# Half B's last projection interleaved, token tile by token tile, with steps of half A's channel mixer; attention outputs stored from ScalarE's queue

## The chip, the cores and the metric

The kernel runs on one NeuronCore of a Trainium2 chip. The metric is the device time of one execution in microseconds (us), the median of several runs. Five instruction streams run side by side and meet only at semaphores: PE (TensorE, the matrix multiplies), DVE (VectorE), ACT (ScalarE), POOL (GpSimd) and SP (SyncE, which here issues all data transfers). Each stream is executed in the order in which the program lists it.

## The reference, cut to what matters

A two-layer trunk is applied to 1024 prompt rows and 64 sample rows of width 1024. Each layer is a mixer, then a gated feed-forward block (the "channel mixer"), each with a residual and a layer norm:

```python
x = layer_norm(DEEPNORM_ALPHA * x + mix, ln1_w[layer], ln1_b[layer])
x = layer_norm(DEEPNORM_ALPHA * x + swiglu(x, ffn_w_in[layer], ffn_w_out[layer]), ln2_w[layer], ln2_b[layer])

def swiglu(x, w_in, w_out):
    gate, up = jnp.split(x @ w_in, 2, axis=-1)      # 1024 -> 2 x 2816
    return (jax.nn.silu(gate) * up) @ w_out         # 2816 -> 1024
```

Layer 0's mixer is a recurrent one, layer 1's is chunk-band softmax attention with 16 heads of 64, whose output goes through one projection, `mix = attention(x) @ w_o` (1024 x 1024). The change lies wholly in layer 1.

## The kernel before, in words

**Two halves.** The rows are split into half A (384 prompt rows and the 64 sample rows, 448 columns, index 0) and half B (the other 640 prompt rows, index 1, five token tiles of 128). The halves run out of step, so that the vector work of one lies beside the matrix work of the other. In layer 1, half A is already in its channel mixer while half B is in attention.

**Precision.** Every product is made of three matmuls: operands are kept as a rounded high part and a low part (`wh`/`wl` for a weight, `xh`/`xl` for an activation), and hi*hi, hi*lo and lo*hi are summed. `load_w` (L93 to 108) loads a weight of 512 KB into a raw buffer `wr` (two of them), ACT rounds it to `wh` (L100), and DVE and POOL share the subtraction that gives `wl` (L105, L107). There are four buffers each for `wh` and `wl` (`self.WB = 4`).

**Channel mixer of half A.** `ffn` (L906) is a Python generator. Each step j of 22 loads two weights, runs 2 x 24 matmuls of 128x448 (`gemm_ws`, L123 to L125), and forms one hidden tile `hh`/`hl`. After steps 3, 7, 11, 15, 17 and 21 (`GROUPS`), the hidden tiles so far go through the output matrix (`tsg`), whose matmuls are 128x512 and whose sums DVE adds into `acc` (L823, L825). `next(f)` asks for one step more.

**Projection of half B.** `proj` runs `tsg` twice, for the second and then the first half of the inner dimension. Each `tsg` has two column halves (nh) of 512, and per token tile and nh 12 matmuls (L134, L135, L137). The second `tsg` got `after`, the layer norm of a tile: it loaded all four of its weights first, and then ran tile by tile both column halves and `after(i)`.

**Layer norm.** Per tile: DVE takes statistics (L871, L873), POOL forms the reciprocal deviation `rstd` (L875, L876), DVE scales (L879, L884 for the second column half), ACT and POOL finish the first column half (L881, L882), and PE transposes both halves, four 128x128 blocks each (L889). Then `sums` (L950 to 1003) splits the transposed tile into high and low parts and builds, on DVE and ACT, the operand sums S1 to S4 that half B's own channel mixer (`s_ffn`) multiplies; that mixer computes two row halves in a form with fewer products.

**Order.** The program is recorded and then scheduled by a planner: every engine gets a fixed list, mainly in the order of the code, with later work pulled ahead where the planner's model sees an engine free. Buffers are given out in that order too. At the end of layer 1's attention of half B, `run` (L1455 to 1469) goes on with `for j in f`; at j = 15 (`JM`) it loads the attention outputs `og_d` and the residual, and calls `self.proj(1, acc1, "w_o", ...)`. Steps 16 to 21 of half A's mixer come after it, then `s_ffn`. The attention of a pair of heads ends with its output tile `o` (DVE, L1312) stored to `og_d` from SP's queue (L1316).

Of the kernel before, what the change touches and what calls it, by code (L numbers as in the profile page):

```python
# [82 lines left out]
class Kern:  # L83
# [712 lines left out]
            self.nc.sync.dma_start(acc[i][:m], src[self.base[hf] + t0 : self.base[hf] + t0 + m, :])  # L796
        return acc

    def tsg(self, hf, acc, wsrc, pairs, hi, lo, first, after=None, packed=None):

        def load(nh):
            ws = []
            for pr in pairs:
                h_, l_ = self.load_w(wsrc(nh, pr), [128, 2, 512])
                ws += [(h_[:, j, :], l_[:, j, :]) for j in range(2)]
            return ws

        kts = [2 * pr + j for pr in pairs for j in range(2)]  # L810

        def part(ws, nh, i, t0, m):
            two = packed and m == 64
            ps = self.bank()
            if two:
                self.gemm_ts(ps, ws, packed, None, kts, lambda x: x[:, 0:128])
            else:
                self.gemm_ts(ps[:m], ws, hi, lo, kts, lambda x: x[:, t0 : t0 + m])
            a = acc[i][:m, 512 * nh : 512 * nh + 512]
            if first:  # L820
                self.V.scalar_tensor_tensor(a, a, ALPHA, ps[:m], op0=ALU.mult, op1=ALU.add)
            else:
                self.V.tensor_tensor(a, a, ps[:m], op=ALU.add)  # L823
            if two:
                self.V.tensor_tensor(a, a, ps[m:], op=ALU.add)  # L825

        if after is None:
            for nh in range(2):
                ws = load(nh)
                for i, t0, m in self.toks(hf):  # L830
                    part(ws, nh, i, t0, m)
        else:
            ws = [load(nh) for nh in range(2)]
            for i, t0, m in self.toks(hf):
                for nh in range(2):
                    part(ws[nh], nh, i, t0, m)
                after(i)
# [6 lines left out]
        self.G.tensor_copy(xs[:, :, 64:128], xt.lo[:, :, SMP:])  # L844
        return lambda kt: xs[:, kt, :]

    def proj(self, hf, acc, wname, after, pool=None):

        xt = self.xt[hf]
        packed = self.pack(pool) if pool else None  # L850
        for i, g in enumerate((1, 0)):
            self.tsg(hf, acc, lambda nh, pr: self.a[wname][nh, pr], (2 * g, 2 * g + 1), xt.h, xt.l, i == 0, after if i else None, packed)

    def layer_norm(self, hf, acc, which, layer, out=None, transpose=True, sums=None):

# [347 lines left out]
    def attention(self, hf, hp, sp, parts=None):  # L1203


        nc, V, A, G, T = self.nc, self.V, self.A, self.G, self.T
        n, xt, c0 = self.N[hf], self.xt[hf], self.base[hf]
# [14 lines left out]
        o = sp.tile([128, n], F32, tag="o", name="o", bufs=1)  # L1222
# [6 lines left out]
        for h in range(2):  # L1229
# [18 lines left out]
            for grp in groups:  # L1248
                ng, first = len(grp), grp[0][2][0][0]
# [5 lines left out]
                for i, (q0, m, keys) in enumerate(grp):  # L1255
# [21 lines left out]
                    for j0 in range(0, len(keys), 4):  # L1277
# [10 lines left out]
                        for dst, src, kk in ops:  # L1288
                            t3 = tp[:kk].rearrange("p (j q) -> p j q", q=128)[:, src, :m]
                            hi = ph[:kk, dst, :m]  # L1290
# [22 lines left out]
        if hf == 0:  # L1313
            self.split(xt.h(hp), xt.l(hp), o)
        else:
            nc.sync.dma_start(self.og_d[hp], o)  # L1316


    def run(self):
        nc, tc, a = self.nc, self.tc, self.a  # L1320
# [26 lines left out]
        g = self.gla(0, sc, 1, None)  # L1347
# [25 lines left out]
        g = self.gla(1, sc, 1, gS)  # L1373
# [9 lines left out]
        hp = es_a.enter_context(tc.tile_pool(name="hpA", bufs=1))  # L1383
# [21 lines left out]
        with tc.tile_pool(name="qp", bufs=1) as qp:  # L1405
            self.vproj(0, qp, 2)
            for hp in range(8):
                if hp == self.JX:
                    with tc.tile_pool(name="yr1", bufs=1, side="right") as yp:
                        self.load_xt(1, self.yg_d, (4, 5, 6, 7, 0, 1, 2, 3), pool=yp)  # L1410
                    acc1 = self.load_acc(1, a["x"], accp)
# [9 lines left out]
        hp = es_b.enter_context(tc.tile_pool(name="hpB", bufs=1))  # L1421
        f = self.ffn(1, 0, acc1, hp, lambda: self.layer_norm(1, acc1, "ln2", 0, xd(1)))
# [11 lines left out]
        with tc.tile_pool(name="at1", bufs=1, side="right") as atp:  # L1434
# [13 lines left out]
            hp = es_a.enter_context(tc.tile_pool(name="hpA1", bufs=1))  # L1448
            outA = lambda t0, m: a["y_s"] if t0 == SMP else a["y_p"][t0 : t0 + m, :]
            f = self.ffn(0, 1, acc0, hp, lambda: self.layer_norm(0, acc0, "ln2", 1, outA, transpose=False))  # L1450
# [7 lines left out]
        for j in f:  # L1458
            if j == self.JM:
                accp = self.ctx.enter_context(tc.tile_pool(name="accB1", bufs=1, side="right"))  # L1460
                self.xt[1] = self.xt_tiles(xbp, 1)
                with tc.tile_pool(name="yr2", bufs=1, side="right") as yp:
                    self.load_xt(1, self.og_d, (4, 5, 6, 7, 0, 1, 2, 3), pool=yp)
                self.paired = True
                acc1 = self.load_acc(1, self.x_d, accp)
                xs, sums = self.s_operands(self.ctx.enter_context(tc.tile_pool(name="sx", bufs=1, side="right")),
                                           self.ctx.enter_context(tc.tile_pool(name="st", bufs=1, side="right")))
                self.proj(1, acc1, "w_o", self.layer_norm(1, acc1, "ln1", 1, sums=sums))
        es_a.close()
        hp = self.ctx.enter_context(tc.tile_pool(name="hpB1", bufs=1))  # L1470
        outB = lambda t0, m: a["y_p"][PA + t0 : PA + t0 + m, :]
# [86 lines left out]
```

## Time and profile before

| what | value |
|---|---|
| median of 3 runs | 3194.87 us (3192.62 to 3196.44) |
| the profiled execution | 3194.15 us, of which the span from first to last instruction is 3192.4 us |
| PE busy | 3038.5 us, 95% of the span |
| DVE, POOL, ACT busy | 2029.7, 1342.5, 1263.7 us |
| mean granted TensorE clock | 0.968 of full speed |
| end of half B's attention (last L1307 matmul) | about 2486 us |
| half B's projection with its layer norm | about 2549 to 2647 us |
| steps 16 to 21 of half A's mixer | about 2647 to 2739 us |
| first matmul of half B's mixer (L1044) | 2749.7 us |

The page cuts the span into 40 slices of 79.8 us; a digit is a busy share in tenths, and the row PEclk is the clock that TensorE was granted. Stages named here by time can be looked up there: slices 30 and 31 hold the end of the attention, slice 32 the projection.

### The profile page before, as it was taken

The page shows a single profiled execution, that of the slowest core. Times are in us where ns is not written, and L with a number is a line of the kernel's source. Part 1 is how long each engine was busy: PE and PEld are TensorE (multiplying, and loading weights), DVE is VectorE, ACT ScalarE, POOL GpSimd, SP SyncE. Part 2 cuts the span into 40 slices and gives each one's busy share as a digit, 9 for nine tenths or more (in the row PEclk, how much of TensorE's full clock was granted, in tenths as well). Part 3 has the DMA queues.
Part 4 walks back from the last instruction along what each step waited for, and adds up shares of the span by engine and source line. Part 5 has one row for each costly group of instructions (what it writes and reads, how often), then busy time and mean ns, then how long its engine had stood idle before and what let it go on. Part 6 is the DMA issues. An engine that isn't in the chain of part 4 may idle for free.

```text
span 3192.4 us, 50089 instructions
## 1 busy us (share of the span) xinstructions
PE 3038.5 (95%) x17468; PEld 2695.8 (84%) x17468; DVE 2029.7 (64%) x4953; ACT 1263.7 (40%) x2753; POOL 1342.5 (42%) x1461
## 2 busy tenths in 40 slices
PE   8999998899999999999999999999997979899998
PEld 7878887688888878888899898999996858799987
DVE  4677885979888664555553635445665556766667
ACT  4454553434444324244342223454444323333332
POOL 2354433535454334343332323345455323555444
PEclk9989999799999999999999999999997889999999
DMA  6553444434433248344432325764543413322121
GB/s 194 145 156 110 113 119 111 142 102 122 134 103 109 88 151 271 112 135 119 119 97 93 108 74 197 210 193 147 146 130 98 142 34 113 108 86 100 54 93 73
DMA packets 297341, 395.10 MB, mean 124 GB/s; under 512 B 125377, under 2 KB 218425, under 8 KB 297089
## 3 DMA queue, kind: packets, MB, share of 16 engines
q1 hardware_dynamic: 297088, 391.90, 41.1%
q8 instruction: 138, 2.26, 0.3%
q14 instruction: 115, 0.93, 0.1%
HBM read 319.44 MB, written 75.51 MB: 124 GB/s over the span
## 4 chain that ended last, share of the span: by engine, by line
PE 76%; DVE 9%; DMA 6%; issue 4%; POOL 3%; ACT 2%; SPq 1%; POOLq 0%; DVEq 0%; ACTq 0%
PE gps L123 11%; PE gps L124 11%; PE gps L125 11%; PE gps L134 7%; PE gps L135 7%; PE gps L137 6%; PE gps L1044 2%; PE gps L1045 2%; PE gps L1046 2%; PE op L1307 2%; PE tp L1281 2%; DVE x L550 1%; PE sps L1265 1%; DVE t L548 1%; PE ps L621 1%
## 5 line engine op out<-in xcount | busy, mean ns | idle before, releaser
L107 POOL TENSOR_TENSOR wl<-wr,wh 128x384 fp32r<-128x384 f32 (+2 forms) x289 | 510.7, 1771 | 690.3 <-ACT wh L100 632.6
L123 PE MATMUL gps<-xh,wh 128*128 128x320 f32 (+1 forms) x2188 | 751.1, 344 | 11.0 <-ACT xh L214 5.9
L124 PE MATMUL gps<-xl,wh 128*128 128x320 f32 (+1 forms) x2188 | 749.2, 342 | 0.6 <-DVE xl L215 0.6
L125 PE MATMUL gps<-xh,wl 128*128 128x320 f32 (+1 forms) x2188 | 746.8, 342 | 1.3 <-DVE wl L105 0.7
L100 ACT CAST wh<-wr 128x1024 fp32r<-128x1024 f32 x352 | 367.0, 1048 | 514.4 <-PE gps L124 155.6
L105 DVE TENSOR_TENSOR wl<-wr,wh 128x640 fp32r<-128x640 f32 (+2 forms) x289 | 284.0, 983 | 257.7 <-ACT wh L100 255.6
L123 PEld LDWEIGHTS gps<-xh,wh 128*128 128x128 f32 x2188 | 417.1, 191 | 33.6 <-ACT wh L100 6.1
L125 PEld LDWEIGHTS gps<-xh,wl 128*128 128x128 f32 x2188 | 416.4, 190 | 20.5 <-DVE wl L105 1.5
L124 PEld LDWEIGHTS gps<-xl,wh 128*128 128x128 f32 x2188 | 416.6, 190 | 18.5 <-DVE xl L215 1.0
L1276 POOL TENSOR_SCALAR s<-s,mx 128x640 f32<-128x640 f32 (+5 forms) x144 | 203.0, 1410 | 268.0 <-DVE mx L1275 226.4
L134 PE MATMUL gps<-wh,xh 128*128 128x512 f32 x661 | 263.1, 403 | 2.9 <-ACT xh L1074 2.5
L137 PE MATMUL gps<-wh,xl 128*128 128x512 f32 x661 | 260.9, 401 | 4.8 <-DVE xl L215 4.8
L135 PE MATMUL gps<-wl,xh 128*128 128x512 f32 x661 | 263.3, 400 | 2.0 <-DVE wl L105 2.0
L134 PE MATMUL gps<-wh,hh 128*128 128x512 f32 x572 | 226.6, 397 | 0.3 <-DVE acc L823 0.3
L135 PE MATMUL gps<-wl,hh 128*128 128x512 f32 x572 | 226.1, 396 | 0.0
L823 DVE TENSOR_TENSOR acc<-acc,gps 128x512 f32<-128x512 f32 (+1 forms) x216 | 143.6, 679 | 101.6 <-PE gps L137 95.6
L137 PE MATMUL gps<-wh,hl 128*128 128x512 f32 x484 | 189.4, 397 | 2.8 <-DVE hl L929 2.8
L548 DVE TENSOR_TENSOR t<-lt,x 16x48 f32<-16x48 f32 (+9 forms) x540 | 151.8, 281 | 39.4 <-DMA lt<-l_d 29.0
L1274 ACT ACTIVATE s<-s,mx 128x640 f32<-128x640 f32 (+5 forms) x144 | 96.4, 670 | 163.7 <-DVE mx L1273 158.3
L137 PEld LDWEIGHTS gps<-wh,xl 128*128 128x128 f32 x661 | 126.1, 191 | 32.5 <-DVE xl L215 5.3
L134 PEld LDWEIGHTS gps<-wh,xh 128*128 128x128 f32 x661 | 126.5, 192 | 31.9 <-ACT xh L1074 2.9
L550 DVE TENSOR_TENSOR x<-x,t 16x48 f32<-16x48 f32 (+9 forms) x540 | 144.9, 268 | 11.0
(355 smaller groups left out, 6339.3 us busy)
## 6 DMA issues: line engine op xcount, KB each, us to landing
wr<-in_w_fi SPq DMA_DIRECT2D x176, 512.0 KB
wr<-in_w_fo SPq DMA_DIRECT2D x88, 512.0 KB
wr<-in_w_in SPq DMA_DIRECT2D x44, 512.0 KB
wr<-in_w_qk SPq DMA_DIRECT2D x32, 512.0 KB
qs<-qd SPq DMA_DIRECT2D x32, 320.0 KB
wr<-in_w_om SPq DMA_DIRECT2D x16, 512.0 KB
wr<-in_w_v SPq DMA_DIRECT2D x16, 512.0 KB
vd<-vh SPq DMA_DIRECT2D x16, 512.0 KB
```

The costliest lines, as they stand in the source:

```text
L100: self.A.copy(hi, raw)
L105: self.V.tensor_tensor(lo[:, :h], raw[:, :h], hi[:, :h].bitcast(F32), op=ALU.subtract)
L107: self.G.tensor_tensor(lo[:, h:], raw[:, h:], hi[:, h:].bitcast(F32), op=ALU.subtract)
L123: self.T.matmul(ps, hi[:, kt, :], xh, start=(kt == 0), stop=False)
L124: self.T.matmul(ps, hi[:, kt, :], xl, start=False, stop=False)
L125: self.T.matmul(ps, lo[:, kt, :], xh, start=False, stop=(kt == nk - 1))
L134: self.T.matmul(ps, xh, wh, start=(i == 0), stop=False)
L135: self.T.matmul(ps, xh, wl, start=False, stop=(lo is None and i == n - 1))
L137: self.T.matmul(ps, cols(lo(kt)), wh, start=False, stop=(i == n - 1))
L548: V.tensor_tensor(tv, lt[:, j, w:16].unsqueeze(2).to_broadcast([m, r, w]), x[:, 0, j, 0:w].unsqueeze(1).to_broadcast([m, r, w]), op=ALU.mult)
L550: V.tensor_tensor(x[:, 0, w:16, 0:w], x[:, 0, w:16, 0:w], tv, op=ALU.add)
L1276: G.tensor_scalar(s[:m, :nk], s[:m, :nk], mx[:m, 3:4], None, op0=ALU.mult)
```

## The change

`tsg` and `proj` take a new argument `between`. Where it is given, both passes of the projection run column half by column half (outer loop nh), each with two weights loaded ahead of it; and in the last of the four (second pass, nh = 1) each token tile's 12 matmuls are followed in the code by `between()` and then by the tile's layer norm. `between` is `next(f, None)`, one step of half A's channel mixer, so that steps 16 to 20 (with the output product after step 17) are written between the five tiles. Step 21 and what follows stay behind the projection. The store of the attention output moves from SP's queue to ScalarE's.

```diff
-    def tsg(self, hf, acc, wsrc, pairs, hi, lo, first, after=None, packed=None):
+    def tsg(self, hf, acc, wsrc, pairs, hi, lo, first, after=None, packed=None, between=None):
...
-        if after is None:
+        if after is None or between:
             for nh in range(2):
                 ws = load(nh)
                 for i, t0, m in self.toks(hf):
                     part(ws, nh, i, t0, m)
+                    if after and nh:
+                        between()
+                        after(i)
         else:
             ws = [load(nh) for nh in range(2)]
             for i, t0, m in self.toks(hf):
...
-            nc.sync.dma_start(self.og_d[hp], o)
+            nc.scalar.dma_start(self.og_d[hp], o)
...
-                self.proj(1, acc1, "w_o", self.layer_norm(1, acc1, "ln1", 1, sums=sums))
+                self.proj(1, acc1, "w_o", self.layer_norm(1, acc1, "ln1", 1, sums=sums), between=lambda: next(f, None))
```

What the planner makes of it is seen first on PE, in the last part of half B's projection. In the rows below, `gps` is a PSUM tile, `acc` a token tile of half B (27558 the first, 27560 the second), `wh`/`wl` a weight, `xh1`/`xl1` half B's activations, `xh0`/`xl0` half A's. Before, the projection's matmuls and the transposes of the tiles (L889) stood alone:

```order
L137 MATMUL gps_27793<-wh_27774,xl1_27521 128x512
L889 MATMUL gps_27825<-ident_71,acc_27558 128x128 x4
L134 MATMUL gps_27838<-wh_27753,xh1_27520 128x512
...
L134 MATMUL gps_27852<-wh_27774,xh1_27520 128x512
L889 MATMUL gps_27818<-ident_71,acc_27558 128x128 x4
L135 MATMUL gps_27852<-wl_27775,xh1_27520 128x512
...
L137 MATMUL gps_27852<-wh_27774,xl1_27521 128x512
L889 MATMUL gps_27877<-ident_71,acc_27560 128x128 x4
L889 MATMUL gps_27884<-ident_71,acc_27560 128x128 x4
L134 MATMUL gps_27914<-wh_27753,xh1_27520 128x512
```

Now, at the same place (transposes at L893):

```order
L137 MATMUL gps_27849<-wh_27844,xl1_27521 128x512
L123 MATMUL gps_27877<-xh0_69,wh_27865 128x448
...
L125 MATMUL gps_27905<-xh0_69,wl_27873 128x448
L893 MATMUL gps_27947<-ident_71,acc_27558 128x128 x4
L893 MATMUL gps_27954<-ident_71,acc_27558 128x128 x4
L134 MATMUL gps_27967<-wh_27837,xh1_27520 128x512
...
L137 MATMUL gps_27967<-wh_27844,xl1_27521 128x512
L123 MATMUL gps_27995<-xh0_69,wh_27983 128x448
```

Between a tile's last matmul and its transposes there now stand the 48 matmuls of a step of half A's mixer, and 12 instead of 24 matmuls of the projection follow before the next step. The number of instructions is the same; the first 12,054 rows of PE's list, and all rows from shortly behind the first products of half B's mixer on, are alike.

The second place is POOL, in the same stretch. Before, it had three layer-norm instructions per tile and nothing else there:

```order
L107 TENSOR_TENSOR wl_27775<-wr_27772,wh_27774 128x512
L875 TENSOR_SCALAR rstd_27812<-mv_27810 128x1
L876 TENSOR_TENSOR rstd_27812<-rstd_27812,mhalf_72 128x1
L882 TENSOR_TENSOR acc_27558<-acc_27558,gb_27580 128x512
L875 TENSOR_SCALAR rstd_27871<-mv_27869 128x1
L876 TENSOR_TENSOR rstd_27871<-rstd_27871,mhalf_72 128x1
L882 TENSOR_TENSOR acc_27560<-acc_27560,gb_27580 128x512
```

Now the weights of the mixer's steps stand between them:

```order
L107 TENSOR_TENSOR wl_27873<-wr_27870,wh_27872 128x384
L879 TENSOR_SCALAR rstd_27941<-mv_27939 128x1
L880 TENSOR_TENSOR rstd_27941<-rstd_27941,mhalf_72 128x1
L886 TENSOR_TENSOR acc_27558<-acc_27558,gb_27580 128x512
L107 TENSOR_TENSOR wl_27984<-wr_27981,wh_27983 128x384
L107 TENSOR_TENSOR wl_27991<-wr_27988,wh_27990 128x384
L879 TENSOR_SCALAR rstd_28135<-mv_28133 128x1
```

The low parts of a later step's weights wait behind a tile's layer norm on POOL, and the other way round.

The third place is the store in the end of the attention. On ACT, before:

```order
L1274 ACTIVATE s_26534,mx_26535<-s_26534,mx_26535 128x640
L1311 COPY ot_26348<-op_26335 64x256
L1291 CAST xh1_23955<-tp_26522 128x4x128
L1274 ACTIVATE s_26557,mx_26558<-s_26557,mx_26558 128x640
L1291 CAST xh1_23955<-tp_26541 128x4x128
```

and now:

```order
L1278 ACTIVATE s_26534,mx_26535<-s_26534,mx_26535 128x640
L1315 COPY ot_26348<-op_26335 64x256
L1320 DMA og_d_90<-o_26046 128x640
L1295 CAST xh1_23955<-tp_26522 128x4x128
L1278 ACTIVATE s_26557,mx_26558<-s_26557,mx_26558 128x640
```

The store waits for DVE's `o`, which follows the copy `ot`, and the cast of the next pair's probabilities stands behind it. SP's list is the same as before without its eight stores, but for the two loads of the next layer norm's weights (`gb`, L860), which move from behind the weights of step 17's output product to behind the third of the four weights of the last output product.

More of the change, by code (lines that the diff above doesn't have):

```diff
@@ L845, in pack, with proj @@
         return lambda kt: xs[:, kt, :]
-    def proj(self, hf, acc, wname, after, pool=None):
+    def proj(self, hf, acc, wname, after, pool=None, between=None):
         xt = self.xt[hf]
@@ L851, in proj @@
         for i, g in enumerate((1, 0)):
-            self.tsg(hf, acc, lambda nh, pr: self.a[wname][nh, pr], (2 * g, 2 * g + 1), xt.h, xt.l, i == 0, after if i else None, packed)
+            self.tsg(hf, acc, lambda nh, pr: self.a[wname][nh, pr], (2 * g, 2 * g + 1), xt.h, xt.l, i == 0, after if i else None, packed, between)
     def layer_norm(self, hf, acc, which, layer, out=None, transpose=True, sums=None):
```

## The prediction

> **What bounds the kernel now.** I read the profile page first, for the engine shares and the 40 slices; then the windows of the stages that the change touches; then PE's waits there; then the timelines of the instructions in those waits.
>
> ```profile
> PE 3038.5 (95%) x17468; PEld 2695.8 (84%) x17468; DVE 2029.7 (64%) x4953; ACT 1263.7 (40%) x2753; POOL 1342.5 (42%) x1461
> ...
> PE   8999998899999999999999999999997979899998
> ...
> PEclk9989999799999999999999999999997889999999
> ```
>
> PE is busy for 95% of the span, so time can only be won where PE idles or runs at a lowered clock. The worst slice is the 33rd (digit 7, clock 7): it holds half B's last projection with its layer norm. The windows cut that place by stage. Their columns are: window, length, then busy us (instructions) of PE, weight loads, DVE, ACT and POOL, the granted clock, the DMA share and GB/s.
>
> ```profile
> 2549.00:2582.90 33.90, 33.90 (x146) 27.02 (x144) 15.00 (x20) 5.46 (x6) 10.02 (x6) 1.00 0.28 82
> 2582.90:2647.30 64.40, 34.82 (x133) 27.71 (x133) 44.79 (x88) 17.61 (x37) 19.51 (x19) 0.78 0.10 32
> 2647.30:2679.80 32.50, 32.50 (x147) 28.98 (x146) 20.34 (x38) 11.21 (x22) 7.38 (x6) 0.92 0.34 112
> 2679.80:2738.70 58.90, 58.90 (x281) 52.34 (x279) 34.83 (x52) 15.87 (x21) 19.27 (x15) 1.00 0.32 104
> 2738.70:2749.70 11.00, 0.01 (x1) 0.02 (x1) 9.73 (x14) 2.81 (x3) 8.65 (x6) 0.62 0.30 112
> 2582.90:2738.70 155.80, 126.22 (x557) 109.03 (x556) 99.96 (x177) 44.69 (x79) 46.16 (x39) 0.89 0.23 76
> ```
>
> In the 64.40 us of the projection's last part PE works 34.82 us at clock 0.78. The steps behind it (32.50 and 58.90 us) have PE full, with DVE at 20.34 and 34.83 us. The change mixes these two kinds of work. Then PE stands idle for 11.00 us before half B's mixer. PE's waits in the stretch, as idle us, count and longest:
>
> ```profile
> PE gps L889 <- POOL acc L882: 13.1, 2, 7.2
> PE gps L889 <- DVE acc L884: 12.0, 2, 7.6
> PE gps L1044 <- ACT wh L1018: 11.0, 1, 11.0
> PE gps L889 <- issue: 4.4, 1, 4.4
> ```
>
> The transposes L889 wait 13.1 + 12.0 + 4.4 = 29.5 us, once per token tile, for the layer norm; that is all of the idle time of the stretch (155.80 − 126.22 = 29.58). The third row, the wait for a weight of half B's mixer (L1018), stands behind everything that is moved.
>
> **The most there is to gain.** I price PE's work of the stretch at full clock by these rows: four steps of half A's mixer with 192 matmuls of 128x448, 88 matmuls of 128x512 of the output product, and one group of transposes.
>
> ```profile
> 2679.90:2718.60 38.70, 38.70 (x193) 35.92 (x192) 18.82 (x28) 11.35 (x15) 13.40 (x8) 1.00 0.36 114
> 2718.80:2738.60 19.80, 19.80 (x88) 16.16 (x86) 15.78 (x24) 4.24 (x6) 5.87 (x7) 1.00 0.25 83
> 2593.80 0.60 PE L889 MATMUL gps<-ident,acc 128*128 128x128 f32 x4
> ```
>
> That is 38.70/192 = 0.2016 us, 19.80/88 = 0.225 us and 0.60 us per four transposes; a projection matmul costs 33.90/146 = 0.232 us (first window above). The stretch holds 6 steps of 48 matmuls (58.1 us), 132 matmuls of output products (29.7), 96 projection matmuls (22.3) and 10 groups of transposes (6.0): 116.1 us. So 155.8 − 116.1 = **39.7 us** can go: 29.6 of waiting and 10.1 of lowered clock. PE's list is the same before and behind the stretch, so nothing else on PE changes.
>
> **Part 1: the layer norm gets a cover.** A tile's chain from its last sum to its transposes, in the timelines of DVE, POOL and ACT (start, duration, instruction; in brackets the idle time before):
>
> ```profile
> 2582.94 0.69 DVE L823 TENSOR_TENSOR acc<-acc,gps 128x512 f32<-128x512 f32 x1 [1.39 <-PE gps L137]
> 2583.66 0.69 DVE L871 BATCH_NORM_STATS2 bs<-acc 128x6 f32<-128x512 f32 x1
> 2584.39 0.21 DVE L873 BATCH_NORM_AGGREGATE mv<-bs 128x2 f32<-128x12 f32 x1
> 2586.51 0.75 DVE L884 SCALAR_TENSOR_TENSOR acc<-acc,rstd,gb 128x512 f32<-128x512 f32 x1 [0.46 <-POOL rstd L876]
> 2584.70 0.74 POOL L875 TENSOR_SCALAR rstd<-mv 128x1 f32<-128x1 f32 x1 [4.07 <-DVE mv L873]
> 2585.52 0.95 POOL L876 TENSOR_TENSOR rstd<-rstd,mhalf 128x1 f32<-128x1 f32 x1
> 2587.31 1.27 POOL L882 TENSOR_TENSOR acc<-acc,gb 128x512 f32<-128x512 f32 x1 [0.83 <-ACT acc L881]
> 2586.51 0.72 ACT L881 ACTIVATE acc<-acc,rstd 128x512 f32<-128x512 f32 x1 [8.07 <-POOL rstd L876]
> ```
>
> From 2582.94 to the end of L882 at 2587.31 + 1.27 = 2588.58 it takes 5.64 us. In the new order the 48 matmuls of a step, 48 x 0.2016 = 9.7 us, stand between. The chain fits with 4.0 us to spare, and the 29.6 us go if nothing else delays it. With no wait as long as those the clock should stay up, which gives the 10.1 us.
>
> But the chain now meets the step's own vector work. Between the first tile and the end of step 21 PE has 58.1 + 44 x 0.225 + 6.0 + 60 x 0.232 = 87.9 us of work. DVE has there the 44.79 us of the projection, less five sums of 0.69 that come earlier, and the 20.34 and 18.82 us of the steps: 80.5 us, or 92%. Queues at 92% make some results late by more than 4.0 us. Bounds: nothing, and a wait as long as now in every tile (29.6 us). What can be late: on DVE the scaling L884 waits for `rstd` (0.46 us above), and the `wl` and `ht` of the step stand queued behind it; on POOL `rstd` can now stand behind a low part of 1.65 us (row in part 2). Five tiles, 8.3 us of DVE's time, of which the spare 4.0 us of each chain take most. I take 3.5 us on PE; a tile's statistics and scaling stand ahead of the step's vector work in DVE's list, which speaks for a small value.
>
> **Part 2: the weights.** Two of the four `wh`/`wl` buffers hold projection weights through the five tiles, so the steps have two left: a weight can be prepared only while the other is being used. The load itself has its own two raw buffers. One raw load, one cast and one low part (POOL's share, the longer one):
>
> ```profile
> 2636.87 3.44 DMA wr<-in_w_fi
> 2699.44 1.05 ACT L100 CAST wh<-wr 128x1024 fp32r<-128x1024 f32 x1 [3.66 <-PE gps L125]
> 2700.57 1.65 POOL L107 TENSOR_TENSOR wl<-wr,wh 128x384 fp32r<-128x384 f32 x1 [3.50 <-ACT wh L100]
> ```
>
> A buffer freed is usable again after 1.05 + 1.65 plus a hand-over of 0.08 = 2.8 us. The other weight covers it with 24 matmuls, 4.8 us, or 7.6 us with a tile's projection matmuls in between. So 2.0 us are to spare. Bounds: nothing, and load, cast and low part exposed for all twelve weights, 12 x (3.44 + 1.05 + 1.65) = 73.7 us, which would need the raw buffers to be empty too. I take 1.5 us: four weights in the worst places, each behind a layer-norm instruction of 1.27 us on POOL that eats part of the spare 2.0.
>
> The two loads of `gb` (1024 x 128 floats, 512 KB, as a weight) move on SP's queue behind the third weight of the last output product; two loads of 3.44 us are 6.9 us, and step 21 with 24 matmuls lies ahead of their use, 9.7 + 5.4 = 15.1 us. I take 0; uncovered they would cost 6.9.
>
> **Part 3: DVE and POOL beside each other.** POOL's weight work now runs beside the layer norm. What that does to an instruction can be read already: L884 takes 0.75 us in the row above, and here 1.80.
>
> ```profile
> 2628.19 1.80 DVE L884 SCALAR_TENSOR_TENSOR acc<-acc,rstd,gb 128x512 f32<-128x512 f32 x1
> 2628.18 1.26 POOL L882 TENSOR_TENSOR acc<-acc,gb 128x512 f32<-128x512 f32 x1 [0.83 <-ACT acc L881]
> ```
>
> It began together with L882 on POOL, and 0.75 + 1.26 = 2.01 is nearly its duration: the two run almost one after the other. The low estimate is nothing, since DVE's 99.96 us hold such losses already; the high one is one such loss (1.05) for each of ten layer-norm halves and twelve weights, 23 us, all on PE's path. I take 2.0 us, two of them reaching PE, since most end in the spare times above.
>
> [...]
>
> **Part 4: the store on ACT.** SP issued it in 319 to 1095 ns, in the middle 327; its neighbours on SP show whether PE waited for it.
>
> ```profile
> L1316 SPq DMA_DIRECT2D og_d<-o x8: 319/327/1095, 2089.6 to 2487.2; - x8
> 2410.70 0.38 SPq L1221 DMA_DIRECT2D vt<-vd  x1
> 2411.61 0.33 SPq L1316 DMA_DIRECT2D og_d<-o  x1
> 2415.57 0.45 SPq L1239 DMA_DIRECT2D ks<-kd  x1
> ```
>
> The next `ks` load is issued 3.6 us behind the store, so SP was not short of time, and taking the store away wins nothing at PE. On ACT it stands between the copy `ot` and the next cast, and waits for DVE's `o`.
>
> ```profile
> 2450.15 0.37 ACT L1311 COPY ot<-op 64x256 f32<-64x256 f32 x1
> 2451.26 0.58 ACT L1291 CAST xh<-tp 128x512 fp32r<-128x512 f32 x1 [0.74 <-PE tp L1281]
> 2450.56 0.42 DVE L1312 TENSOR_TENSOR o<-op,ot 64x256 f32<-64x256 f32 x1 [0.34 <-ACT ot L1311]
> ```
>
> `o` ends at 2450.98 and the cast starts at 2451.26: 0.28 us are free, the issue takes 0.33, so 0.05 us are lost, up to 0.8 at the slowest issue. Eight stores: 0.4 us, at most 6.6, and only where the cast is what PE waits for. I take 0.2.
>
> **Sum.** −39.7 + 3.5 + 1.5 + 2.0 + 0.2 = −32.5 us. On the profiled 3194.15 that is 3161.65, and the median of the runs lies 0.7 above the profiled execution: **3162 us**. The 11.0 us before half B's mixer stay, with the work ahead of them only moved earlier.
>
> **On the clock.** The 10.1 us hang on short waits not lowering the clock. The nearest row against that is a stretch of the attention:
>
> ```profile
> 2430.00:2450.00 20.00, 16.58 (x76) 13.92 (x74) 9.73 (x31) 8.93 (x22) 9.31 (x8) 0.64 0.31 66
> ```
>
> PE works 16.58 of 20 us there, and its clock is 0.64. So many short waits can lower it. If the new stretch ran like this, the 10.1 us would stay, and A would end at 3172. But the projection's waits here average 5.9 us, and the stages with PE full run at 0.92 and 1.00, so I keep the 10.1. [...]
>
> **The rivals.**
>
> *B: DVE with POOL becomes the bound.* For it speaks the 92% above and the 1.80 us. If the two engines excluded each other altogether, the stretch could not be shorter than 99.96 + 46.16 = 146.1 us: 9.7 us gained, 3185. Against the full form speaks that PE was full in 2679.80 to 2718.60 with 18.82 + 13.40 us in 38.70, and that DVE's sums and the steps' products read PSUM. Half of the way between this and the forecast is the likelier form, 3174.
>
> *C, slower: the two weight buffers.* Were a step's weight started only when its buffer comes free, its whole load would be exposed: 73.7 us in place of the 39.7 won, 34 us slower, 3229. It decides from 39.7/12 = 3.3 us per weight on. For it: only two buffers are left to the steps. Against it: the raw buffers are separate, so that the 3.44 us are fetched ahead, and the 2.8 us that remain are below 3.3 and covered by 4.8.
>
> *D, no change: the waits only move.* If the layer norm were issued behind the step's vector work on DVE, its 5.64 us would start only when the step ends, and PE would wait 5 x 5.9 us as now, at the same low clock: 3194. Against it speaks that place in DVE's list.
>
> That the change doesn't do what it says can be left out: the order of PE's instructions shows the 48 matmuls between tile and transposes.
>
> **How the numbers follow.** Forecast A has 0.60; its own range is 3156 (the four costs a microsecond in all) to 3172 (clock not regained). B has 0.25, of which 0.05 the full form. C has 0.07, D 0.08. The range 3155 to 3179 holds A and most of B, leaving out C, D and B's full form, about 0.2. A measurement of this kernel can tell 0.2%, 6.4 us, from no change. A and B are faster by more than that, so faster has 0.85, same 0.08 and slower 0.07.
>
> **What would show it.** In the new profile's windows, the stretch from the first tile's sums to half B's first matmul (L1048 now) without its 11 us should be some 123 us long and PE over 93% busy, at a clock of 0.97 or more. Transposes (L893) should wait under 4 us in all; B shows as waits of PE on DVE's `hl`, `wl` or `acc` and a DVE share above 95%; C as waits on `wh` (L100) or `wl` by a microsecond or more each; D as five waits of the transposes. The wait for `wh` at L1022 should stay near 11 us. The casts of L1295 should show idle time behind the store of some tenths at most. The prediction is wrong if PE's idle time in the stretch is above 20 us, if the clock there is below 0.9, or if the time outside the stretch moves by more than 3 us.

## The result, and the profile after

The changed kernel takes 3156.36 us (median of 4 runs, 3153.94 to 3157.09) against 3193.74 us before on the same chip (3192.37 to 3196.44): a ratio of 0.9881, 95% interval 0.9863 to 0.9898, 37.4 us less. On another chip, run again for the last group of experiments, it took 3160.61 us, 0.9908 (0.9893 to 0.9923) of before.

The profile page after, with the rows that answer to those shown of before: engine shares, PE's slices and the granted clock.

```profile
PE 3031.0 (96%) x17468; PEld 2687.8 (85%) x17468; DVE 2025.3 (64%) x4953; ACT 1264.7 (40%) x2753; POOL 1340.7 (42%) x1461
...
PE   8999999799999999999999999999998899899998
...
PEclk9989999899999999999999999999998899999999
```

The 33rd slice, which had PE at 7, now has 9, with the clock at 9. (The prediction gave that slice's clock before as 7; the row has 8 there, and 7 two slices earlier, in the attention.) The 35th slice, 2682 to 2760 us, has PE at 8: it holds the 10.7 us that are still waited. The windows after: the projection's first 144 matmuls; the stretch from there to the end of half A's last output product; the wait before half B's mixer; and, inside the stretch, the part from the first step to the end of step 21. Columns as before: length, busy us (instructions) of PE, weight loads, DVE, ACT and POOL, clock, DMA share, GB/s.

```profile
2545.92:2579.70 33.78, 33.78 (x146) 27.23 (x145) 15.00 (x20) 5.33 (x6) 10.02 (x6) 1.00 0.27 82
2579.70:2697.46 117.76, 115.96 (x556) 100.43 (x555) 99.36 (x177) 44.13 (x79) 45.93 (x39) 1.00 0.31 100
2697.46:2708.12 10.66, 0.00 (x1) 0.00 (x0) 8.67 (x14) 2.14 (x3) 8.08 (x6) 0.66 0.34 123
2590.72:2677.31 86.59, 84.79 (x422) 75.27 (x420) 74.68 (x135) 35.70 (x66) 37.75 (x31) 1.00 0.34 110
```

The stretch that took 155.80 us takes 117.76. PE is busy for 115.96 us of it (98.5%) at clock 1.00. Neither DVE's work (99.96 us before, 99.36 after) nor POOL's (46.16, 45.93) has become less or slower; it lies under more matmuls. What PE still waits for from the projection to the end of the kernel, its largest waits:

```profile
PE gps L1048 <- ACT wh L1022: 10.7, 1, 10.7
PE gps L1048 <- DVE c L1063: 3.3, 2, 2.8
PE gps L134 <- ACT xh L1078: 2.5, 1, 2.5
PE gps L893 <- DVE acc L888: 1.0, 1, 1.0
PE gps L893 <- POOL acc L886: 0.8, 2, 0.5
PE gps L1050 <- DVE wl L1023: 0.8, 1, 0.8
PE gps L1048 <- DVE c L1061: 0.5, 1, 0.5
```

The transposes (L893) wait 1.0 + 0.8 us in place of 29.5. The weight of half B's mixer (L1022) is waited for as before. At the start of that mixer PE now waits 0.8 us for DVE's `wl` and 0.5 and 2.8 us for its sums `c`; before, it waited there 1.4 us for a second weight and 1.2 us for `c`. This is taken up below. The wait of 2.5 us (L134) lies late in the mixer and is there before too.

**Where the time went.** From one profiled execution to the next, the projection's first matmul falls anywhere between 2540 and 2556 us in the kernels of this study, although PE's list of matmuls ahead of it is the same. I found no cause for that; it is larger than several of the effects, so I count from that matmul on. The table gives, in us, the length up to the end of half A's last output product, PE's idle and busy time in it, the wait for half B's first matmul, and what follows from there to the last instruction. The kernels are described below.

| kernel | to end of product | PE idle | PE busy | wait | rest | sum | against before |
|---|---|---|---|---|---|---|---|
| before | 189.55 | 29.58 | 159.97 | 10.98 | 442.72 | 643.25 | |
| the change | 151.54 | 1.80 | 149.74 | 10.66 | 446.68 | 608.88 | −34.4 |
| the change, again | 151.41 | 1.81 | 149.60 | 10.82 | 446.78 | 609.01 | −34.2 |
| store_only | 189.20 | 29.83 | 159.37 | 10.99 | 442.69 | 642.88 | −0.4 |
| steps_only | 151.37 | 1.82 | 149.55 | 10.85 | 446.76 | 608.98 | −34.3 |
| halves_only | 182.89 | 23.85 | 159.04 | 10.97 | 444.29 | 638.15 | −5.1 |
| lag | 162.92 | 11.10 | 151.82 | 10.98 | 444.35 | 618.25 | −25.0 |
| lag_order | 163.79 | 11.85 | 151.94 | 10.97 | 444.31 | 619.07 | −24.2 |
| norm_first | 171.85 | 17.69 | 154.16 | 10.99 | 445.10 | 627.94 | −15.3 |
| dve_more | 153.06 | 3.79 | 149.27 | 9.52 | 448.27 | 610.85 | −32.4 |
| dve_much | 162.71 | 8.06 | 154.65 | 7.78 | 458.33 | 628.82 | −14.4 |
| one_buffer | 167.92 | 13.11 | 154.81 | 9.86 | 445.64 | 623.42 | −19.8 |
| a_halves | 151.36 | 1.83 | 149.53 | 1.65 | 452.67 | 605.68 | −37.6 |
| a_halves_wp | 151.41 | 1.80 | 149.61 | 1.61 | 452.90 | 605.92 | −37.3 |

So the change wins 27.8 us of waiting and 10.2 us of clock up to the end of the product, 0.3 us at the wait, and gives 4.0 us back in half B's mixer: −34.4 us.

### The profile page after: what moved, and what is told of

The parts are those of the page before. It is cut to its first block, busy times and chain, and to the rows that moved or that the text cites. A ratio compares the mean times of both kernels' runs of the same rounds, so it can differ in the third digit from the quotient of the medians.

```text
span 3154.8 us, 50085 instructions
## 1 busy us (share of the span) xinstructions
PE 3031.0 (96%) x17468; PEld 2687.8 (85%) x17468; DVE 2025.3 (64%) x4953; ACT 1264.7 (40%) x2753; POOL 1340.7 (42%) x1461
## 3 DMA queue, kind: packets, MB, share of 16 engines
q10 hardware_dynamic: 1152, 2.62, 0.2%
## 5 line engine op out<-in xcount | busy, mean ns | idle before, releaser
L107 POOL TENSOR_TENSOR wl<-wr,wh 128x384 fp32r<-128x384 f32 (+2 forms) x289 | 509.1, 1766 | 665.5 <-ACT wh L100 607.4
L125 PE MATMUL gps<-xh,wl 128*128 128x320 f32 (+1 forms) x2188 | 742.4, 340 | 0.7 <-DVE wl L105 0.7
L125 PEld LDWEIGHTS gps<-xh,wl 128*128 128x128 f32 x2188 | 413.9, 189 | 19.1 <-DVE wl L105 1.5
L134 PE MATMUL gps<-wh,xh 128*128 128x512 f32 x661 | 260.4, 399 | 2.5 <-ACT xh L1078 2.5
L134 PE MATMUL gps<-wh,hh 128*128 128x512 f32 x572 | 224.9, 397 | 0.3 <-DVE acc L824 0.3
L134 PEld LDWEIGHTS gps<-wh,xh 128*128 128x128 f32 x661 | 125.4, 190 | 30.8 <-ACT xh L1078 2.9
```

The lines of the kernel that those rows point to most:

```text
L107: self.G.tensor_tensor(lo[:, h:], raw[:, h:], hi[:, h:].bitcast(F32), op=ALU.subtract)
L125: self.T.matmul(ps, lo[:, kt, :], xh, start=False, stop=(kt == nk - 1))
L134: self.T.matmul(ps, xh, wh, start=(i == 0), stop=False)
```

## The experiments

**The two edits apart.** `store_only` is the kernel before with this edit alone; `steps_only` is the change without it.

```diff
-            nc.sync.dma_start(self.og_d[hp], o)
+            nc.scalar.dma_start(self.og_d[hp], o)
```

> The kernel before with only the store moved to ScalarE's queue. Theory: within 1 us of before, 3194 us. Rival (the store on SP holds up loads): 3190 us or less. Second rival (the casts behind it wait, 0.8 us for each of eight): 3200 us.

> The changed kernel with the store put back on SP's queue; everything else as in the change. Theory (the whole gain comes from the steps that cover the layer norm, the store is worth 0.2 us): 3156 us, 37 us below before, as the full change. Rival (the store on SP holds up loads of the attention, so taking it away pays): the gain shrinks by 3 us or more, to 3160 us or above, and PE's waits between 2089 and 2487 us grow.

`store_only` took 3192.75 us, 0.9998 (0.9987 to 1.0009) of before; `steps_only` 3153.63 us, 0.9870 (0.9854 to 0.9886). The store does nothing that can be measured, and the steps make the whole gain. Its issues on ACT in the change (least, middle and most ns):

```profile
L1320 ACTq DMA_DIRECT2D og_d<-o x8: 326/326/345, 2086.9 to 2484.9; - x8
```

At 326 to 345 ns none takes as long as the longest on SP.

**The order by column halves alone.** `halves_only` is the change with a function between the tiles that does nothing.

```diff
-                self.proj(1, acc1, "w_o", self.layer_norm(1, acc1, "ln1", 1, sums=sums), between=lambda: next(f, None))
+                self.proj(1, acc1, "w_o", self.layer_norm(1, acc1, "ln1", 1, sums=sums), between=lambda: None)
```

> The changed kernel in which the function between the tiles does nothing: column half by column half, the layer norm after each tile's last 12 matmuls, all steps of half A behind the projection. Theory (the cover makes the gain): the layer norms follow at DVE's pace, 44.79/5 = 9.0 us per tile, so the last part takes 60 matmuls (13.9 us) + 45 us = 59 in place of 64.4, the clock stays low, and the time is 3189 us. Rival (the order by column halves makes the gain, since only 12 matmuls are left behind the first layer norm): 3165 us or less.

It took 3187.20 us, 0.9973 (0.9960 to 0.9986). Its window from the first projection matmul to the end of the product:

```profile
2544.05:2726.94 182.89, 159.04 (x701) 135.20 (x699) 115.82 (x197) 49.65 (x85) 57.15 (x45) 0.92 0.23 80
```

PE idles for 23.85 us there and the clock is 0.92, as before the change (0.91). The column halves alone save 5 us, and the theory's 3189 is right within 2 us. The other 29 us of the change need something in front of the transposes.

**Another cover.** `lag` and `lag_order` start from the kernel before. The steps of half A stay behind the projection, and a tile's layer norm is written behind the next tile's 24 matmuls. `lag` takes the tile with the next lower number for the one before, but the tiles are visited in the order 2, 0, 3, 1, 4; so it normalises some tiles before their sums are complete, and what it computes is wrong. `lag_order` keeps the right order, and the conclusions rest on it. Its edit:

```diff
+            late, todo = int(hf == 1 and getattr(self, "late", False)), []
             for i, t0, m in self.toks(hf):
                 for nh in range(2):
                     part(ws[nh], nh, i, t0, m)
+                todo.append(i)
+                if len(todo) > late:
+                    after(todo.pop(0))
+            for i in todo:
                 after(i)
...
+                self.late = True
                 self.proj(1, acc1, "w_o", self.layer_norm(1, acc1, "ln1", 1, sums=sums))
+                self.late = False
```

> The kernel before in which a tile's layer norm is written behind the next tile's 24 matmuls; the steps of half A stay behind the projection. Theory (the layer norm needs a cover that has little work of DVE's own): 24 matmuls are 5.6 us against a chain of 5.6 us, but DVE needs 9.0 us per tile against 6.8 us on PE, so DVE sets the pace, 45 us in place of 64.4, and some clock comes back: 3174 us, with DVE over 90% busy in that part. Rival (any matmuls between a tile and its transposes would do): the waits go as in the change, 3160 us or less.

> The run lag took the tile with the next lower number, but the tiles of this projection are visited in the order 2, 0, 3, 1, 4, so some were normalised before their sums were complete; here it is the tile visited before. Nothing else differs: each layer norm is written behind the next tile's matmuls, the steps of half A behind the projection. PE's list has 12, 30, 6 and 0 matmuls in front of the transposes of the later tiles. Theory (DVE's pace, 9.0 us per tile, and an uncovered last tile): 45 us in place of 64.4 us and some clock, 3174 us. Rival (24 matmuls of the projection itself are cover enough; only the last tile waits, as in lag, 11 us): 3163 us.

They took 3163.38 us, 0.9907 (0.9887 to 0.9928), and 3165.72 us, 0.9912 (0.9888 to 0.9936). By the trace `lag_order` is 24.2 us below before. The theory had said 3174 and the rival 3163, so the rival's time is the nearer one, and some 70% of the gain (24.2 of 34.4 us) is to be had without mixing the two kinds of work. The windows of `lag_order` from the 144th projection matmul to the last tile's first transposes, the part of it from the first transposes on, and the whole up to the end of the output product; then PE's waits in it:

```profile
2573.70:2613.60 39.90, 28.05 (x133) 22.84 (x133) 37.37 (x70) 14.67 (x29) 17.93 (x19) 0.85 0.18 62
2584.72:2613.60 28.88, 17.03 (x86) 14.04 (x85) 28.81 (x56) 13.51 (x28) 14.19 (x14) 0.80 0.21 74
2539.93:2703.72 163.79, 151.94 (x701) 129.81 (x699) 113.97 (x197) 49.78 (x85) 53.81 (x45) 0.96 0.26 90
```

```profile
PE gps L894 <- POOL acc L887: 6.3, 1, 6.3
PE gps L894 <- DVE acc L889: 5.6, 1, 5.6
```

The first three tiles wait no more; the last two wait 6.3 and 5.6 us. The mechanism of the theory shows all the same: DVE is busy for 28.81 of 28.88 us at the end, so it sets the pace there. Its size was off: DVE has 37.37 us of work there, not 45, because some of it lies earlier, and the part takes 39.9 us. What the steps add over this cover, by PE's lists, is matmuls in front of the last tiles' transposes too, where `lag_order` has 6 and none.

**The place of the transposes.** `norm_first` is the change with two lines swapped, so that the same work is mixed, and the layer norm is written first.

```diff
-                        between()
                         after(i)
+                        between()
```

> The changed kernel with the two calls swapped: a tile's layer norm is written ahead of the step of half A, not behind it. The same work is mixed, but PE's list has the transposes of the first and the last tile directly behind the tile's last matmul, and 22 to 24 matmuls of 128x448 in front of those of the other three. Theory (what stands between a tile's last sum and its transposes decides): two full waits of 5.6 us, three of 5.6 - 4.8 = 0.8 us, and some 3 us of clock: 17 us more than the change, 3173 us. Rival (mixing the two kinds of work is enough, wherever the transposes stand): 3157 us.

It took 3173.39 us, 0.9931 (0.9909 to 0.9954), as the theory had it (3173), 17 us more than the change and 19 by the trace. PE's waits for the transposes, as sum, count and longest:

```profile
PE gps L893 <- POOL acc L886: 9.4, 3, 5.7
PE gps L893 <- DVE acc L888: 8.3, 1, 8.3
```

The transposes of the first tile wait 5.72 us and of the last 8.28, those with some matmuls in front 1.07, 2.62 and none. Mixing is not enough; the matmuls have to stand between a tile's sums and its transposes.

**How near DVE is to the bound.** `dve_more` adds statistics instructions on DVE that nothing uses, four for each tile; `dve_much` adds twelve (`range(6)`).

```diff
                 sums(i, *halves)
+                for _ in range(2):
+                    for j in range(2):
+                        V.bn_stats(bs[:, j, :], a[:, 512 * j : 512 * j + 512])
```

> The changed kernel with four statistics instructions of 0.69 us more on DVE behind each tile's sums (results not used): 20 x 0.69 = 13.8 us. Theory (DVE at 92% between the first tile and the end of step 21, so 7.4 us are free): 94.3 us of work in 87.9 us, at least 6 us slower than the change, 3163 us, with waits of PE on DVE. Rival (DVE is far from being the bound there): 3157 us or less.

> As dve_more with twelve statistics instructions more per tile: 60 x 0.69 = 41.4 us on DVE. Theory (DVE sets the pace once its free time is used up; by dve_more, where 13.8 us cost about 2, some 12 us are free): 41.4 - 12 = 29 us more than the change, 3185 us, with PE waiting for DVE between the tiles. Rival (most of these instructions find idle time further on, since nothing waits for them): 3165 us or less.

`dve_more` took 3159.74 us, 0.9890 (0.9869 to 0.9911), 2.0 us more than the change by the trace: less than the 6 us of the theory. The intervals of the two kernels overlap, so the times alone would not tell it from none. `dve_much` took 3177.94 us, 0.9960 (0.9945 to 0.9975), where the change took 3160.61 on the same chip: 17 us more, between the theory (29) and the rival. The windows from the first step to the last of step 21, first `dve_more`, then `dve_much`:

```profile
2592.15:2680.27 88.12, 84.33 (x421) 75.37 (x420) 80.61 (x145) 33.98 (x61) 35.50 (x31) 1.00 0.31 107
```

```profile
2589.37:2687.14 97.77, 89.71 (x422) 78.33 (x421) 96.20 (x173) 34.17 (x61) 31.35 (x31) 0.95 0.26 88
```

In the change DVE is busy for 74.68 of 86.59 us there (86%); in `dve_more` for 80.61 of 88.12 (91%), where PE waits 3.8 us in place of 1.8 up to the end of the product; in `dve_much` for 96.20 of 97.77 (98%), where it waits 8.1 us. In both, the trace puts most of the transposes' waits to POOL's `acc` (L886), which comes behind DVE's statistics of the tile. So DVE does become the bound, from somewhere above 91% on. 11.6 us of the 19.8 that the trace shows for `dve_much` come behind the product, in half B's mixer (458.33 against 446.78 in the change, run again on that chip).

**The weight buffers.** `one_buffer` loads one weight more ahead of the last column half and keeps it, so that the steps have one pair of buffers.

```diff
                 ws = load(nh)
+                keep = self.load_w(wsrc(0, pairs[0]), [128, 2, 512]) if after and nh else ()
...
+                for t in keep:
+                    self.V.tensor_copy(self.ap.tile([128, 2], F32, tag="mv", name="mv", bufs=2)[:, 0:1], t[:, 0, 0:1].bitcast(F32))
```

> The changed kernel with one more weight loaded ahead of the last column half and kept until its end (it is read only there), so that the steps between the tiles have one wh and one wl buffer in place of two. Theory (a buffer freed is usable again after 2.8 us, which the other weight's 24 matmuls cover; without the other buffer each of the 12 weights of steps 16 to 20 and the product behind 17 exposes it, unless a tile's 12 matmuls stand there): up to 12 x 2.8 = 34 us more than the change, 3180 to 3190 us, with waits of PE on wh or wl. Rival (weights are prepared far enough ahead in any case): 3160 us or less.

It took 3175.41 us, 0.9950 (0.9935 to 0.9965), 15 us more than the change beside it. PE's waits up to the end of the product:

```profile
PE gps L123 <- ACT wh L100: 5.7, 6, 1.0
PE gps L125 <- DVE wl L105: 4.5, 4, 2.7
PE gps L134 <- ACT wh L100: 1.9, 2, 1.0
```

Now weights are waited for; these three groups are twelve waits with 12.1 us. But a `wh` costs at most 1.0 us, about the 1.05 of the cast; the low part is used only by the third matmul of each three (L125), and its waits are 4.5 us in four. The 2.8 us that I took for a freed buffer are not all on the path. The order of PE's list differs a little too, since the planner saw fewer buffers. Even with a single buffer the change keeps more than half of its gain.

**The same edit in a second place.** A wait of 7.8 to 11.0 us before half B's mixer stood in all kernels so far. In `a_halves` the change's own edit is used in a second place: half A's last output product.

```diff
-        if after is None or between:
+        if after is None or between or (hf == 0 and self.gp2):
...
                     if after and nh:
-                        between()
+                        if between:
+                            between()
                         after(i)
```

`a_halves_wp` adds to it:

```diff
-                pool, tag, bufs = (((self.wp, kind, self.WB),) * 4 + ((hp, kind, 1), (accA, "acc", 4)))[n % 6]
+                pool, tag, bufs = (((self.wp, kind, self.WB),) * 4 + ((hp, kind, 1), (accA, "acc", 4) if n > 5 else (self.wp, kind, self.WB)))[n % 6]
```

> The changed kernel in which half A's last output product also runs column half by column half, with its layer norm behind the second half, so that two of its four weights are free some 10 us before its end. Theory (the 10.7 us before half B's mixer are a wait for weight buffers, whose casts and differences can begin only when the product's last tile is done): the first weights are prepared during the product, the wait shrinks to 2 to 4 us, 3149 us. Rival (the wait is for DVE, ACT and POOL, which work off half A's layer norm in the same time): the wait stays and the time is 3156 us, or more, since the layer norm now begins later.

> The changed kernel with half A's last output product column half by column half, as in a_halves, and in half B's mixer the sixth wh and wl in a weight buffer of the pool in place of one of half A's residual tiles, which comes free only after its layer norm and store. Theory (in a_halves the second wait, 6.2 us, is for that store): it shrinks to 2 us or less, some 4 us less than a_halves and 7 us less than the change, 3149 us beside 3156. Rival (it is DVE, ACT and POOL that are late with half A's layer norm): no gain over a_halves, 3153 us.

The expectation for the change itself, which ran beside `a_halves_wp`:

> The changed kernel itself, on the chip of the three others. All theories: 0.988 of before, and the same trace again: from the projection's first matmul to the end of the last output product 151.5 us, then 10.7 us of waiting, then 446.7 us to the end.

`a_halves` took 3151.19 us, 0.9862 (0.9842 to 0.9883). `a_halves_wp` took 3156.62 us, 0.9892 (0.9876 to 0.9909), and the change on that chip 3160.61. PE's waits from the end of the product on, first of `a_halves`, then of `a_halves_wp`:

```profile
PE gps L1049 <- ACT wh L1023: 7.8, 2, 6.2
PE gps L1049 <- DVE c L1062: 2.6, 1, 2.6
```

```profile
PE gps L1049 <- ACT wh L1023: 6.4, 2, 4.8
PE gps L1049 <- DVE c L1062: 2.6, 1, 2.6
```

The first wait falls from 10.7 to 1.65 us, but a second one of 6.2 us turns up 24 us later, for the next weight. With the other buffer it is still 4.8 us, so that buffer was not the main cause. It was worth 1.4 us: by the 400th matmul of half B's mixer `a_halves_wp` is 1.4 us ahead, and the sums of the parts (605.9 against 605.7 us) agree only because 1.6 us are lost again behind it, as much as a late wait costs in clock in some profiles and not in others (last section). The rest of the wait is open between theory and rival. The chain that ended last before the 4.8 us, in `a_halves_wp` (start, length, step), holds both POOL's layer norm of half A and the store that the theory named:

```profile
2715.61 1.79 POOL acc L887
...
2717.41 2.88 DMA out_dram<-acc
...
2720.30 3.52 DMA wr<-in_w_fi
...
2723.98 0.64 POOL wr L1029
...
2729.73 1.23 POOL wr L1032
...
2730.98 1.05 ACT wh L1023
```

The load of a raw weight (`wr`) waits there for the store of a residual tile, since the kernel gives every second pair of raw weights the room of residual tiles as well; the edit moved only `wh` and `wl`, and no run moved `wr`. Of 9.0 us won at one place `a_halves` loses 6.0 again (452.67 against 446.68). What is left is 3.2 us by the trace. Both versions are clearly faster than the kernel before. Against the change they are not shown to be faster: the median is 4 us lower on the one chip, which agrees with the trace, but the intervals overlap.

## Why the prediction was right

The forecast was 3162 us; the time is 3156.4, at the lower end of the forecast's own range (3156 to 3172), where the four costs come to a microsecond in all. By its steps:

- **The most there is to gain, 39.7 us, from idle time and clock.** PE's work of 116.1 us at full clock was measured as 115.96. The waits fell by 27.8 us and the clock gave back all of its 10.1 us: the clock of the stretch went from 0.89 to 1.00.
- **Part 1, 3.5 us for late layer norms.** Measured 1.8 us at the transposes. I had DVE at 92%; it is at 86%, since part of its work of the projection lies ahead of the first step and part behind step 21. In `dve_more`, at 91%, the transposes wait 3.8 us, so the 3.5 us fit the load that I assumed; it was the load that I had too high.
- **Part 2, 1.5 us for weights.** PE's waits show none for `wh` or `wl` before the end of the product. Even with a single buffer a weight costs 1.0 us on average, not the 2.8 that I took; the low part is needed last (`one_buffer`).
- **Part 3, 2.0 us for DVE beside POOL.** Nothing of it shows between the tiles. But half B's mixer takes 4.0 us more, where I had expected the time to stay, and the sum has no term for that. What was wrong is the sentence that PE's list is the same behind the stretch: in the timelines, the first 126 matmuls of that mixer stand partly in another order, and so do DVE's instructions beside them. Matmul 72 of the mixer ends 4.2 us later, counted from its first, than before; 1.8 us are made up by the 240th, and 1.6 us more are lost at a single wait late in the mixer (next section but one). The last is not the change's doing: `lag_order` loses the same there, and 1.6 us are all that its rest and that of `halves_only` (444.3 us) have above before. Rows of the start of the mixer, first before, then after:

```profile
2752.41 1.27 POOL L882 TENSOR_TENSOR acc<-acc,gb 128x512 f32<-128x512 f32 x1
...
2753.56 1.23 DVE L1019 TENSOR_TENSOR wl<-wr,wh 128x1024 fp32r<-128x1024 f32 x1 [1.41 <-ACT wh L1018]
2754.70 2.44 DVE L879 SCALAR_TENSOR_TENSOR acc<-acc,mv,gb 64x512 f32<-64x512 f32 x2
...
2759.24 0.49 DVE L1059 TENSOR_TENSOR c<-gps,c 128x320 f32<-128x320 f32 x1
...
2762.92 0.69 DVE L1019 TENSOR_TENSOR wl<-wr,wh 128x512 fp32r<-128x512 f32 x1 [2.59 <-DMA out_dram<-acc]
```

```profile
2712.64 2.40 POOL L886 TENSOR_TENSOR acc<-acc,gb 128x512 f32<-128x512 f32 x1
...
2711.66 2.21 DVE L883 SCALAR_TENSOR_TENSOR acc<-acc,mv,gb 64x512 f32<-64x512 f32 x2
2713.80 2.31 DVE L1023 TENSOR_TENSOR wl<-wr,wh 128x1024 fp32r<-128x1024 f32 x1
...
2722.14 0.69 DVE L1023 TENSOR_TENSOR wl<-wr,wh 128x512 fp32r<-128x512 f32 x1 [3.77 <-DMA out_dram<-acc]
2722.75 0.48 DVE L1063 TENSOR_TENSOR c<-gps,c 128x320 f32<-128x320 f32 x1
...
2723.29 0.41 PE L1048 MATMUL gps<-S4h,wh 128*128 128x320 f32 x1 [2.82 <-DVE c L1063]
```

Counted from the mixer's first matmul (2749.68 and 2708.12), the fourth low part `wl` starts at 3.9 us before and at 5.7 us after, and takes 1.23 and 2.31 us. In DVE's list it stood ahead of the scaling of half A's last rows (L879, L883); now it stands behind it, beside POOL's L886, which takes 2.40 us in place of 1.27. PE waits 0.8 us for it. This is the kind of loss that Part 3 meant, in another stage. The larger wait has another place: a later low part must wait until half A's last rows are stored (out_dram), for 2.59 us before and 3.77 after. Before, the sum `c` of L1059 stood ahead of it; now the same sum (L1063) stands behind it, and PE waits 2.8 us for that sum. That these two places in the list are the cause is read from the traces; neither was tried by itself. They are there in all three profiles with the change's order, and DVE's list at the start of the mixer is as before in `lag_order` and `halves_only`, where matmul 240 ends within 0.1 us of before.
- **Part 4, 0.2 us for the store.** `store_only` gave 0.9998 (0.9987 to 1.0009); a term of 0.2 us is too small to be seen.
- **The sum.** −32.5 us forecast; −34.4 by the trace from the projection on. The medians' −37.4 hold some 3 us that lie ahead of the projection (first matmul at 2549.15 before and 2545.92 after), in work that the change does not touch but for the store, and the store alone moves nothing. The second chip gave −31.0. That the sum comes so near is in part luck: within the stretch the terms were 5 us too high (7.0 of parts 1 to 3 against 1.8 of waiting), and behind it 4.0 us were missing.

I had named as a sign of error that the time outside the stretch moves by more than 3 us. It did, by 3.2 us ahead and 4.0 behind, with opposite signs. The first is of the size of what one execution differs from the next; of the second, 2.4 us are a miss of the forecast, and 1.6 us are the late wait's.

Of the rivals, D (the waits only move) is out: the transposes wait 1.8 us. B in its full form, DVE and POOL excluding each other altogether, needs 146.1 us for a stretch that took 117.76. The rows show it for some pairs of instructions and not for others: L884 took 1.80 us beside L882 and 0.75 us by itself, but a sum of PSUM (L823) that lies wholly within a low part on POOL (L107) took 0.69 us, as it does with POOL idle (2582.94, in the prediction). Rows of before:

```profile
2635.18 1.66 POOL L107 TENSOR_TENSOR wl<-wr,wh 128x384 fp32r<-128x384 f32 x1 [5.74 <-ACT wh L100]
2636.17 0.69 DVE L823 TENSOR_TENSOR acc<-acc,gps 128x512 f32<-128x512 f32 x1 [0.20 <-PE gps L137]
```

DVE as the bound is real, but needs 40 us more work (`dve_much`). C, the weight buffers, would have needed 3.3 us per weight; with a single buffer the twelve waits average 1.0.

## What to carry to other kernels

A wait that recurs once per tile is removed by independent work that stands, in the waiting engine's own list, between the tile's last product and its first use: here 29.5 us of waiting became 1.8. Mixed work that stands elsewhere left more than half of the waiting in place (17.7 us, `norm_first`). The idle time and the clock that it costs can be priced from rows before the change, by the same matmuls in a stage where PE is full; here this came out within 0.2 us (116.1 against 115.96). What it does to the helper engines has to be looked for behind the mixed part as well: an engine at 86% hid its lateness between the tiles, while some 2.4 us were lost at the start of the next stage, where the order of the lists had changed too.

## What the runs showed of the hardware

The same wait can cost clock or not. Late in half B's mixer PE waits 2.48 or 2.50 us for ACT in each of seven profiles: `before`, `store_only`, `a_halves`, the change, the change run again, `steps_only` and `lag_order`. The first matmul after it and one 1.5 to 1.7 us later, first before, then after the change:

```profile
3094.32 0.50 PE L134 MATMUL gps<-wh,xh 128*128 128x512 f32 x1 [2.48 <-ACT xh L1074]
3095.81 0.40 PE L134 MATMUL gps<-wh,xh 128*128 128x512 f32 x1
```

```profile
3055.11 0.50 PE L134 MATMUL gps<-wh,xh 128*128 128x512 f32 x1 [2.48 <-ACT xh L1078]
3056.76 0.63 PE L135 MATMUL gps<-wl,xh 128*128 128x512 f32 x1
```

Before, matmuls go on every 0.23 us. After, eight of them run at 0.43 us apiece, 3.4 us in all, and then 0.23 again, which is 1.6 us lost. The granted clock was 0.50 from 3055.90 to 3059.30 us there, and 1.00 before from 3094.32 to 3098.00. Of the other five profiles, `store_only` and `a_halves` look like before; the change run again, `steps_only` and `lag_order` show a slow piece of this kind. What decides between the two is not shown by these rows.

Nor was the lost clock a fixed share of the waiting in these kernels. By the table, PE's busy time lies above the 149.6 us of a full clock by 10.4 us for 29.6 us of waits (before), 9.4 for 23.9 (`halves_only`), 4.6 for 17.7 (`norm_first`) and 2.3 for 11.9 (`lag_order`), and by nothing for 3.8 (`dve_more`); the granted clock over the same length was 0.91, 0.92, 0.95, 0.96 and 1.00. In `one_buffer`, with short waits, none longer than 2.7 us, it lies 5.2 us above, but the clock there was 0.99, which over 167.9 us is 1.7 us; what the other 3.5 us are is open.
